# Five u tiles multiplied before the norm is known, x normalised in turned form, and two gate tiles moved ahead of the S5 blocks

## The chip, the core and the metric

The kernel runs on one core of a Trainium2 chip. TensorE (PE) multiplies matrices from SBUF into PSUM, VectorE (DVE) and ScalarE (ACT) work on elements, GpSimd (POOL) fills constants and issues transfers, and SyncE (SP) issues most transfers. The metric is the device time of one execution in microseconds.

Before the change the median of three runs is 883.1 us (883.09 to 883.79).

## The reference

One decoder block works on 16 meta tokens and 512 tokens of width 1024, in fp32. What matters here is its beginning:

```python
h = jnp.concatenate([meta, x], axis=1)
xn = rmsnorm(h, g_mix_pre[l])          # per token: x * rsqrt(mean(x*x) + eps) * g
proj = xn @ w_in[l]                    # q, k, v, r, a_low, u, z_gla, z_ssm
log_a = log_sigmoid(a_low @ w_gate_up[l] + b_gate[l]) / 16
```

The slices of `proj` then go three ways. q, k, v and `log_a` feed a gated linear attention (GLA) with four heads, whose output is normalised, multiplied by silu(r) and by `w_o_gla`. u feeds an S5 state-space layer with 64 groups of 16 channels, followed by gelu and a gated linear unit. Both results are weighted with sigmoid(z_gla) and sigmoid(z_ssm), added, multiplied by `w_out`, and added to h. A squared-ReLU MLP follows.

The norm scales each token by one number, and a product with `w_in` is linear: (s_t x_t g) @ W = s_t ((x_t g) @ W). A projection can so be multiplied first and scaled by the token's number afterwards.

## The kernel before, in words

**How a product is made.** All matrix products keep fp32 precision with three products of a reduced format (fp32r): an operand is split into a high part (a copy on ACT, `split_hi`, line 159) and a low part (the difference, on DVE), and `mm3` (line 186) adds high x high, high x low and low x high over eight blocks of 128 rows, 24 matmuls for an output tile. Weights come as tiles of 1024 x 128 (`wraw`, 512 KB, three buffers), are split by `split_w_hi` and `split_w_lo` into `whi` and `wlo` (three buffers each), and are the stationary operand. The moving operand is the turned, normalised x: `xh` and `xl`, 128 x 8 x 528, features on the partitions and tokens along the line (512 tokens, then the 16 meta tokens). A projection that needs the meta tokens is made in two halves of 256 and 272 tokens (`HALVES`), any other in one piece of 512. Results of projections take the four PSUM buffers named `mm`; everything else takes the four named `sm`.

**The start (lines 276 to 428).** SP loads the meta rows, four x tiles of 128 tokens (`xt`) and the weights of u tiles 0 to 2 in a fixed order. The gain row is spread over the partitions by PE (`gps`, lines 368 to 376). For each x tile ACT sums the squares (`squared`), four small DVE instructions and one of ACT form the inverse root (`rooted`, `rs`), and DVE multiplies by root and gain (`normed`, `xn`). PE turns the tile (`turned`, eight transposes), ACT takes the high part out of PSUM (`high`) and DVE the low part (`low`). `busy(n)` (line 290) lets PE multiply ones. Between these steps stand the first halves of u tiles 0 to 2 (`u_half`, line 255); their second halves follow at line 425. A finished half is copied from PSUM into `ut` by ACT, and `u_out` (line 270) stores the tile to DRAM for the S5 blocks.

**The stage up to S5 (lines 431 to 792).** The low-rank gate product (`low_rank`, line 458, weights `wa`) reads all of `xh` and `xl`; `gate_up` and `decay_sums` make the running sums of `log_a`: DVE subtracts (line 485) and scans against a mask that is zero at each 128th token (line 487). In the same stretch DVE and ACT compute the S5 layer's tables from its parameters (`chain`, `powers`, `chunk_powers`, `b_bar`). Between the steps stand calls of `slot()` (line 500): each takes the next product of the list `dense`, whose weights were asked for two slots before. The list begins with u tiles 3 to 7, z_ssm tiles 0 to 3 and z_gla tile 4 (lines 545 to 549).

**The blocks (lines 1127 to 1200).** Eight S5 blocks follow, each with a small product (`kernels`), a scan over chunks (`scan`) and an output, and five slots between these steps as work for PE. Blocks 0 to 3 are interleaved with the four GLA heads. The list `dense` goes on with each head's tiles, the other z tiles, the r tiles (`r_slot`, line 1097, which leave `ogh` and `ogl`) and the o tiles (`o_slot`, line 1112, which read all eight of them). z_gla tiles 5, 6 and 7 stand among the r tiles and stay in SBUF; tiles 0 to 4 go to DRAM (`zgd`) and are loaded again.

**What sets the order.** PE's instructions stay in program order up to the MLP (`pinned`). In the start, those of DVE and ACT do too (`InOrder`, `V` and `S` up to line 424). All others are placed by a planner that issues what it takes to be ready; `tc.issue_after` puts an instruction behind another one on the same engine. The order of the loads on SP at the start is fixed in this way (`behind`).

Of the kernel before, what the change touches and what calls it, by code (L numbers as in the profile page):

```python
# [12 lines left out]
ALU = mybir.AluOpType  # L13
# [36 lines left out]
def hybrid_block(ctx: ExitStack, tc: tile.TileContext, io, out: bass.AP):  # L50
# [204 lines left out]
    def u_half(w, ut, q, within=None):  # L255

        a, b = HALVES[q]
        ps = bank("mm")
        feat_tile(w, xh, xl, a, b, ps[:, : b - a], within=within)

        def taken():
            src = ps.rearrange("p (c s) -> p s c", s=T8)
            first = NM // T8 + a // T8
            S.copy(ut[:, :, first : first + 32], src[:, :, :32])
            if q:
                S.copy(ut[:, :, : NM // T8], src[:, :, 32:34])

        return taken
# [9 lines left out]
    gpre = mk(pxt, [P, D], tag="gpre")  # L278
    grow = mk(pxt, [1, D], tag="grow")
    one_row = mk(pxt, [1, P], tag="one_row")  # L280
    V.memset(one_row, 1.0)
    nc.scalar.dma_start(grow, io["g_mix_pre"][0].rearrange("(o d) -> o d", o=1))
    xm = mk(pxt, [P, D], tag="xt", bufs=5)
    xts, raws = [], []
    loaded = nc.sync.dma_start(xm[:NM], io["meta_tokens"])
    ones = mk(pxt, [P, 256], tag="ones")
    V.memset(ones, 1.0)
    idle = bank()

    def busy(n):  # L290

        for _ in range(n):
            PE.matmul(idle[:, :256], ones[:, :P], ones, start=True, stop=True)
# [3 lines left out]

    def x_load(t):
        xt = mk(pxt, [P, D], tag="xt", bufs=5)
        xts.append((xt, P, t * P))  # L300
        return nc.sync.dma_start(xt, io["x"][0, t * P : (t + 1) * P, :])


    for kind, i in (("x", 0), ("x", 1), ("u", 0), ("x", 2), ("u", 1), ("x", 3), ("u", 2)):
        with behind():
            if kind == "x":
                loaded = x_load(i)
            else:
                loaded, raw = raw_w(w_in[:, C_U + i * P : C_U + (i + 1) * P])
                raws.append(raw)  # L310
    xts.append((xm, NM, SEQ))
# [3 lines left out]
    nc.gpsimd.dma_start(vecs, io["vecs"])  # L315
    V, S = InOrder(nc.vector), InOrder(nc.scalar)
    ss = mk(pxt, [P, 5], tag="xss")
    rs = mk(pxt, [P, 5], tag="xrs")
    xns = {}

    def squared(i):
        xt, n, _ = xts[i]
        sq = mk(pxt, [P, D], tag="xsq", bufs=1)
        S.activation(sq[:n], xt[:n], AF.Square, accum_out=ss[:n, i : i + 1])

    def rooted(i):

        n = xts[i][1]
        y, ssum = rs[:n, i : i + 1], ss[:n, i : i + 1]
        parts = mk(pxt, [n, 2], tag="xr_r", bufs=3)  # L330
        a, hm = parts[:, :1], parts[:, 1:]
        S.activation(a, ssum, AF.Sqrt, scale=1.0 / D, bias=epst[:n])
        yield
        V.tensor_scalar(hm, ssum, -0.5 / D, -0.5 * EPS, op0=ALU.mult, op1=ALU.add)
        V.reciprocal(y, a)
        V.scalar_tensor_tensor(a, y, hm, y, op0=ALU.mult, op1=ALU.mult)
        V.scalar_tensor_tensor(y, a, 1.5, y, op0=ALU.add, op1=ALU.mult)

    roots = {}

    def summed(i):
        squared(i)
        roots[i] = rooted(i)
        next(roots[i])

    def normed(i, cols=(0, 512)):
        xt, n, _ = xts[i]
        if i not in xns:
            xns[i] = mk(pxt, [P, D], tag="xn", bufs=3)
            next(roots[i], None)  # L350
        xn = xns[i]
        for c in cols:
            cc = slice(c, c + 512)
            V.scalar_tensor_tensor(xn[:n, cc], xt[:n, cc], rs[:n, i : i + 1], gpre[:n, cc], op0=ALU.mult, op1=ALU.mult)

    def turned(i, tag):
        return [turned_tokens(xns[i][: xts[i][1]], xts[i][1], q, tag if isinstance(tag, str) else tag[q]) for q in range(2)]

    def high(i, q, pvs):
        _, n, col = xts[i]  # L360
        split_hi(xh[:, 4 * q : 4 * q + 4, col : col + n], pvs[q])

    def low(i, q, pvs):
        _, n, col = xts[i]
        dst = slice(4 * q, 4 * q + 4)
        V.tensor_sub(xl[:, dst, col : col + n], pvs[q], f32(xh)[:, dst, col : col + n])

    gps = [bank() for _ in range(2)]
    for i, ps in enumerate(gps):
        PE.matmul(ps, one_row, grow[:, i * 512 : (i + 1) * 512], start=True, stop=True)  # L370
    busy(2)
    summed(4)
    V.tensor_copy(gpre[:, :512], gps[0])
    normed(4, (0,))
    summed(0)
    S.copy(gpre[:, 512:], gps[1])
    summed(1)
    normed(0)
    t0 = turned(0, "mm")
    busy(2)  # L380
    normed(1)
    hi0 = split_w_hi(raws[0])
    w0 = hi0, split_w_lo(raws[0], hi0)
    high(0, 0, t0)
    high(0, 1, t0)
    t1 = turned(1, "sm")
    high(1, 0, t1)
    high(1, 1, t1)
    for q in range(2):
        low(0, q, t0)  # L390
        low(1, q, t1)
    ut0, ut1, ut2 = (u_tile() for _ in range(3))
    take0 = u_half(w0, ut0, 0)
    summed(2)
    hi1 = split_w_hi(raws[1])
    w1 = hi1, split_w_lo(raws[1], hi1)
    take1 = u_half(w1, ut1, 0)
    normed(2)
    summed(3)
    hi2 = split_w_hi(raws[2])  # L400
    w2_ = hi2, split_w_lo(raws[2], hi2)
    take0()
    normed(3)
    ts = {}
    take2 = u_half(w2_, ut2, 0, within=(1, lambda: ts.update({2: turned(2, "mm")})))
    high(2, 0, ts[2])
    high(2, 1, ts[2])
    normed(4, (512,))
    low(2, 0, ts[2])
    low(2, 1, ts[2])  # L410
    t4 = turned(4, "sm")
    t3 = turned(3, ("mm", "sm"))
    take1()
    for q in range(2):
        high(4, q, t4)
        low(4, q, t4)
    for q in range(2):
        high(3, q, t3)
        low(3, q, t3)
    take2()  # L420
# [16 lines left out]
    mask01 = mk(pga, [P, NT], tag="mask01")  # L437
    G.memset(mask01, 1.0)
    for c in range(0, NT, P):
        G.memset(mask01[:, c : c + 1], 0.0)  # L440
# [40 lines left out]
    def decay_sums():  # L481
        S.activation(ga, ga, AF.Exp, scale=-1.0)
        S.activation(ga, ga, AF.Ln, bias=1.0)
        for h in range(HEADS):
            V.tensor_sub(mn[:, h], mn[:, h], ga[:, h])
            b2 = mk(pga, [P, NT], tag="b2", bufs=2)
            V.tensor_tensor_scan(b2, mask01, mn[:, h], 0.0, op0=ALU.mult, op1=ALU.add)
            nc.gpsimd.dma_start(bd[h], b2)
# [644 lines left out]
    for kind in ("r0", "r1", "z5", "r2", "r3", "z6", "r4", "r5", "r6", "r7", "z7", *(f"o{m}" for m in range(KT))):  # L1133
# [11 lines left out]
    for b, blk in enumerate(blocks):  # L1145
# [22 lines left out]
        slot()  # L1168
# [20 lines left out]
        slot()  # L1189
# [329 lines left out]
def laid_out(np, given):  # L1519
# [9 lines left out]
    for name, (one, two) in (("b_cols", bt), ("c_cols", ct)):  # L1529
        rows[name] = np.stack([np.concatenate([one, two]), np.concatenate([two, one])])  # L1530
    return {**{name: a[name] for name in _INS}, **rows}
# [26 lines left out]
```

## Time and profile before

| | |
|---|---|
| median of three runs | 883.1 us |
| the profiled execution's own time | 883.62 us |
| its span in the trace | 881.9 us |
| instructions | 13276 |
| TensorE clock granted, mean | 0.997 |
| HBM read and written | 141.06 MB, 35.42 MB |

The page of the profile gives, in this order: busy time of each engine; the span in 40 slices; the DMA queues; the chain of work that ended last, followed back from the last instruction; the costliest groups of instructions by line, engine, operation and tile, written out<-in; and the DMA issues. Other views group instructions by line or window, list what an engine waited for, or show them in order of time. Times are microseconds from the span's start. PE is the matmul row of TensorE and PEld its weight loads. L78 is the helper that keeps DVE and ACT in program order, and L60 and L65 are PE's helpers, so groups are told apart by their tiles. The duration of a matmul in a row includes the time it takes to run through, so the pace of a series is read from the starts.

### The profile page before, as it was taken

What the parts mean: (1) busy time and instruction counts of PE and PEld (TensorE: products, weight loads), DVE (VectorE), ACT (ScalarE), POOL (GpSimd) and SP (SyncE); (2) the same over time, 40 slices, a digit from 0 to 9 for tenths busy, and PEclk for the clock granted to TensorE, in tenths of its full rate; (3) what the DMA queues carried; (4) which work ended last, traced back from release to release, by engine and by line L of the source; (5) the groups of instructions that cost most, each with busy time, mean ns of one, the idle gap of its engine ahead of it and who ended that gap; (6) DMA issues with size and microseconds to landing.
All of it is one profiled execution on the core that took longest, in us unless ns stands there. A gap on an engine that the chain in (4) does not pass through costs nothing.

```text
span 881.9 us, 13276 instructions
## 1 busy us (share of the span) xinstructions
PE 869.5 (99%) x4856; PEld 742.5 (84%) x4856; DVE 648.6 (74%) x1148; ACT 437.7 (50%) x731; POOL 124.0 (14%) x224
## 2 busy tenths in 40 slices
PE   8999999999999999999999999999999999999996
PEld 6998989898988888888888888988888888888885
DVE  7989898868778698755445765576666678788886
ACT  6475466767655454434333543333222236665763
POOL 1223022030312213232000001021112100000001
PEclk9999999999999999999999999999999999999998
DMA  9647785555454857558545761589998966856564
GB/s 305 179 126 239 205 196 143 136 134 161 109 166 126 260 130 176 170 161 274 187 143 160 228 178 57 172 288 324 333 305 298 324 244 224 280 190 194 170 209 142
DMA packets 164988, 177.36 MB, mean 201 GB/s; under 512 B 18778, under 2 KB 125306, under 8 KB 164923
## 3 DMA queue, kind: packets, MB, share of 16 engines
q1 hardware_dynamic: 146056, 114.74, 44.8%
q0 software_dynamic: 17696, 57.84, 19.4%
q10 hardware_dynamic: 1170, 3.94, 1.3%
q8 instruction: 38, 0.62, 0.3%
q14 instruction: 28, 0.22, 0.1%
HBM read 141.06 MB, written 35.42 MB: 200 GB/s over the span
## 4 chain that ended last, share of the span: by engine, by line
PE 96%; DVE 2%; ACT 1%; DMA 0%; issue 0%; DVEq 0%; SPq 0%
PE mm L60 73%; PE sm L60 21%; PE sm L65 2%; DMA xt<-in_x_dram 0%; DVE xn L78 0%; DVE wlo L78 0%; ACT xsq L78 0%; DVE c L1483 0%; DVE xl L78 0%; PE mm L65 0%; DVE ede L604 0%; DVE c L1477 0%; ACT xh L78 0%; ACT whi L78 0%; DVEq L1554 0%
## 5 line engine op out<-in xcount | busy, mean ns | idle before, releaser
L160 ACT ACTIVATE whi<-wraw 128x1024 fp32r<-128x1024 f32 x101 | 107.0, 1059 | 236.1 <-PE mm L60 207.9
L175 DVE TENSOR_TENSOR wlo<-wraw,whi 128x1024 fp32r<-128x1024 f32 x101 | 123.4, 1222 | 106.7 <-ACT whi L160 106.5
L60 PE MATMUL mm<-xh,whi 128*128 128x512 f32 (+2 forms) x544 | 182.2, 335 | 0.5 <-ACT xh L78 0.5
L60 PE MATMUL mm<-xl,whi 128*128 128x512 f32 (+2 forms) x544 | 178.6, 328 | 1.1 <-DVE xl L78 1.1
L60 PE MATMUL mm<-xh,wlo 128*128 128x512 f32 (+2 forms) x544 | 178.9, 329 | 0.2 <-DVE wlo L78 0.2
L60 PEld LDWEIGHTS mm<-xh,whi 128*128 128x128 f32 x544 | 102.7, 189 | 10.6 <-issue 1.2
L60 PEld LDWEIGHTS mm<-xl,whi 128*128 128x128 f32 x544 | 102.8, 189 | 10.0 <-DVE xl L78 1.5
L60 PEld LDWEIGHTS mm<-xh,wlo 128*128 128x128 f32 x544 | 102.6, 189 | 9.7 <-DVE wlo L78 0.6
L60 PE MATMUL mm<-hh,whi 128*128 128x512 f32 (+1 forms) x280 | 104.0, 371 | 0.0
L60 PE MATMUL mm<-hl,whi 128*128 128x512 f32 (+1 forms) x280 | 103.8, 371 | 0.0
L60 PE MATMUL mm<-hh,wlo 128*128 128x512 f32 (+1 forms) x280 | 103.8, 371 | 0.0
L1420 DVE TENSOR_TENSOR wlo<-wraw,whi 128x1024 fp32r<-128x1024 f32 x56 | 68.4, 1222 | 20.2 <-ACT whi L1416 20.0
L60 PE MATMUL sm<-wlo,fh 128*128 128x512 f32 x192 | 74.8, 390 | 0.0
L60 PE MATMUL sm<-whi,fl 128*128 128x512 f32 x192 | 74.7, 389 | 0.0
L60 PE MATMUL sm<-whi,fh 128*128 128x512 f32 x192 | 74.7, 389 | 0.0
L1416 ACT ACTIVATE whi<-wraw 128x1024 fp32r<-128x1024 f32 x56 | 58.6, 1048 | 17.2 <-PE mm L60 11.7
L60 PEld LDWEIGHTS mm<-hl,whi 128*128 128x128 f32 x280 | 52.7, 188 | 9.1
L60 PEld LDWEIGHTS mm<-hh,whi 128*128 128x128 f32 x280 | 52.7, 188 | 9.1
L60 PEld LDWEIGHTS mm<-hh,wlo 128*128 128x128 f32 x280 | 52.7, 188 | 8.9
L160 ACT ACTIVATE fh<-f 128x512 fp32r<-128x512 f32 x48 | 30.3, 631 | 45.7 <-PE sm L60 30.6
L60 PE MATMUL mm<-gh,whi 128*128 128x512 f32 x128 | 49.8, 389 | 0.0
L60 PE MATMUL mm<-gl,whi 128*128 128x512 f32 x128 | 49.8, 389 | 0.0
(415 smaller groups left out, 1635.0 us busy)
## 6 DMA issues: line engine op xcount, KB each, us to landing
wraw<-in_w_ff_dram SPq DMA_DIRECT2D x56, 512.0 KB, 4.4
wraw<-in_w_in_dram SPq DMA_DIRECT2D x48, 512.0 KB, 4.1
w2raw<-in_w_ff_dram POOLq DMA_DIRECT2D x16, 1024.0 KB, 8.5
t2d<-w2t POOLq DMA_DIRECT2D x16, 1024.0 KB, 5.8
wraw<-t2d SPq DMA_DIRECT2D x32, 512.0 KB, 3.8
wraw<-in_w_glu_dram SPq DMA_DIRECT2D x16, 512.0 KB, 4.4
M<-kpad POOLq DMA_DIRECT2D x64, 64.0 KB, 2.6
wraw<-in_w_o_gla_dram SPq DMA_DIRECT2D x8, 512.0 KB, 7.9
```

What stands on the lines that cost most here:

```text
L60: ins = nc.tensor.matmul(*args, **kw)
L65: ins = nc.tensor.transpose(*args, **kw)
L160: S.activation(dst, src, AF.Copy, scale=scale)
L175: V.tensor_sub(lo, raw, f32(hi))
L1416: halved = S.activation(bh, raw, AF.Copy)
L1420: V.tensor_sub(bl, raw, f32(bh))
```

## The change

**The start.** The kernel receives x and the meta tokens a second time, already turned (`x_cols0` holds the first 256 tokens, `x_cols1` the rest, features on the partitions), and the gain as columns (`g_cols`). The turned x times the gain is split into `rh` and `rl` (`taken_raw`): ACT writes the high part, DVE the low part. u tiles 0 to 4 are multiplied from these. The x tiles by rows are still loaded, three buffers instead of five, for the sums of squares alone. Their roots are formed in two groups (x tiles 0 and 1; then 2, 3 and meta). `spread` brings a group's roots onto all partitions as a row: ACT makes a diagonal matrix of each column, PE multiplies it with ones, and ACT copies the sum. A finished half of a u tile is multiplied by this row on DVE as it leaves PSUM (`taken`), where ACT copied it before. Turned x is then normalised by column tile (`normed`): DVE multiplies by gain and row, ACT copies the high part, and DVE subtracts for two column tiles at once. PE no longer turns x, and the gain is no longer spread. `busy` runs seven matmuls at the start. u tile 0's weights are loaded and split in pieces.

**Decay sums.** The mask is gone. The scan adds one operand and subtracts the other, and is cut at each 128th token, five scans for a head where there was one scan and one subtraction.

**Slots.** `dense` begins with u tiles 5 to 7, z_ssm tiles 0 to 3 and z_gla tiles 4 to 6, ten entries as before. z_gla tiles 5 and 6 are so computed before the blocks, go to DRAM, and are loaded again at o tiles 5 and 6. Among the r tiles only z tile 7 is left, between r6 and r7. The last S5 block has two slots fewer.

```diff
-    def u_half(w, ut, q, within=None):
+    def u_half(w, ut, q, raw=None, tag="mm", within=None):
...
+                if raw:
+                    V.tensor_mul(to, got, scale_rows[0].rearrange("p (c s) -> p s c", s=T8)[:, :, a // T8 + c : a // T8 + c + n])
+                else:
+                    S.copy(to, got)
...
+    for kind, i in (("u", 1), ("h", 0), ("h", 4), ("x", 0), ("x", 1), ("u", 2), ("x", 2), ("x", 3), ("x", 4), ("u", 3), ("u", 4)):
...
+    def taken_raw(k, a, b):
+
+        g = g8[:, k : k + 1]
+        S.activation(rh[:, k, a:b], xT[:, k, a:b], AF.Copy, scale=g)
+        V.scalar_tensor_tensor(rl[:, k, a:b], xT[:, k, a:b], g, f32(rh)[:, k, a:b], op0=ALU.mult, op1=ALU.subtract)
...
+    def spread(c, cols):
+
+        ps = bank()
+        for j, i in enumerate(range(c.start, c.stop)):
+            n = xts[i][1]
+            dg = mk(pxt, [P, P], tag="diag", bufs=3)
+            S.activation(dg[:n, :n], ident[:n, :n], AF.Copy, scale=rs[:n, i : i + 1])
+            PE.matmul(ps[:, j * P : j * P + n], ones[:n, :P], dg[:n, :n], start=True, stop=True)
+        S.copy(rows[:, cols], ps[:, : cols.stop - cols.start])
+
+    def normed(k):
+        V.scalar_tensor_tensor(xT[:, k], xT[:, k], g8[:, k : k + 1], rows, op0=ALU.mult, op1=ALU.mult)
+        S.copy(xh[:, k], xT[:, k])
+        if k % 2:
+            V.tensor_sub(xl[:, k - 1 : k + 1], xT[:, k - 1 : k + 1], f32(xh)[:, k - 1 : k + 1])
...
+    busy(7)
...
+    product(0, 0, w0)
+    w1 = split_w(raws[1])
+    product(1, 0, w1)
+    for k in range(KT):
+        taken_raw(k, 256, NT)
+    product(0, 1, w0)
+    product(1, 1, w1)
+    early, late = slice(0, 2), slice(2, TT + 1)
+    squared(0)
+    squared(1)
+    rooted(early)
+    w2_ = split_w(raws[2])
+    spread(early, slice(0, 256))
+    take(0, 0)
+    take(1, 0)
+    for i in range(2, TT + 1):
         squared(i)
...
+    rooted(late)
+    product(2, 0, w2_)
+    spread(late, slice(256, NT))
+    take(0, 1)
+    take(1, 1)
+    w3 = split_w(raws[3])
+    product(2, 1, w2_)
+    take(2, 0)
+    for i in range(2):
+        u_out(i, uts[i])
+    uts.extend(u_tile() for _ in range(2))
+    product(3, 0, w3)
+    product(3, 1, w3)
     normed(0)
...
     normed(1)
...
+    take(2, 1)
+    u_out(2, uts[2])
+    w4 = split_w(raws[4])
+    for k in range(2, KT):
+        normed(k)
+    product(4, 0, w4)
+    product(4, 1, w4)
+    for i in (3, 4):
+        for q in range(2):
+            take(i, q)
+        u_out(i, uts[i])
     wa = mk(pg, [P, KT, 32], F32R, tag="wa")
     split_hi(wa[:, :, :16], wraw)
     begun = V.tensor_sub(wa[:, :, 16:], wraw, f32(wa)[:, :, :16])
     V, S = nc.vector, nc.scalar
-    for blk, w, ut in ((0, w0, ut0), (1, w1, ut1), (2, w2_, ut2)):
-        u_half(w, ut, 1)()
-        u_out(blk, ut)
...
-            V.tensor_sub(mn[:, h], mn[:, h], ga[:, h])
             b2 = mk(pga, [P, NT], tag="b2", bufs=2)
-            V.tensor_tensor_scan(b2, mask01, mn[:, h], 0.0, op0=ALU.mult, op1=ALU.add)
+            for c in range(0, NT, P):
+                cc = slice(c, min(c + P, NT))
+                V.tensor_tensor_scan(b2[:, cc], mn[:, h, cc], ga[:, h, cc], 0.0, op0=ALU.add, op1=ALU.subtract)
...
-    for m in range(3, KT):
+    for m in range(5, KT):
         u_slot(m)
     for m in range(4):
         gate_slot(C_ZS, m, zs, early_tile)
-    gate_slot(C_ZG, 4, zg, early_tile)
+    for m in range(4, 7):
+        gate_slot(C_ZG, m, zg, early_tile)
...
-    for kind in ("r0", "r1", "z5", "r2", "r3", "z6", "r4", "r5", "r6", "r7", "z7", *(f"o{m}" for m in range(KT))):
+    for kind in ("r0", "r1", "r2", "r3", "r4", "r5", "r6", "z7", "r7", *(f"o{m}" for m in range(KT))):
...
-        slot()
+        if b < NBLK - 1:
+            slot()
```

More of the change, by code (lines that the diff above doesn't have):

```diff
@@ L307, in hybrid_block @@
                 loaded = x_load(i)
+            elif kind == "h":
+                loaded = nc.sync.dma_start(xT[:, i : i + 4, 256:], io["x_cols1"][:, i : i + 4])
             else:
@@ L321, in squared @@
     def squared(i):
[L322 to L334, printed above, removed]
+        xt, n = xts[i]
@@ L356, in turned @@
[L356 to L370, printed above, removed]
@@ new lines, in normed, with product, take @@
+    def normed(k):
[3 more added lines that the diff above has]
+            V.tensor_sub(xl[:, k - 1 : k + 1], xT[:, k - 1 : k + 1], f32(xh)[:, k - 1 : k + 1])
+    raw = rh, rl
+    uts = [u_tile() for _ in range(3)]
+    takes = {}
+    def product(i, q, w, within=None):
+        takes[i, q] = u_half(w, uts[i], q, raw, within=within)
+    def take(i, q):
+        takes[i, q]()
+    busy(7)
@@ new lines, in hybrid_block @@
+    w0 = tuple(mk(wp, [P, KT, P], F32R, tag=t, bufs=3) for t in ("whi", "wlo"))
+    for k in range(0, KT, 2):
+        kk = slice(k, k + 2)
+        for i in range(2):
+            taken_raw(k + i, 0, 256)
+        split_hi(w0[0][:, kk], raws[0][:, kk])
+        V.tensor_sub(w0[1][:, kk], raws[0][:, kk], f32(w0[0])[:, kk])
+    product(0, 0, w0)
[5 more added lines that the diff above has]
+    product(1, 1, w1)
@@ L378, in hybrid_block @@
+    product(3, 0, w3)
+    product(3, 1, w3)
     normed(0)
-    t0 = turned(0, "mm")
-    busy(2)
     normed(1)
[L382 to L416, printed above, removed]
```

108 lines of the change are left out of this document (51 added, 57 removed).

## The prediction

> **What bounds the kernel now.** I read the page's first and fourth parts, then the waits of PE, then windows, then the first 50 us in order of time. Busy time and the chain that ended last, from the page:
>
> ```profile
> PE 869.5 (99%) x4856; PEld 742.5 (84%) x4856; DVE 648.6 (74%) x1148; ACT 437.7 (50%) x731; POOL 124.0 (14%) x224
> ...
> PE 96%; DVE 2%; ACT 1%; DMA 0%; issue 0%; DVEq 0%; SPq 0%
> ```
>
> PE's waits over the whole span (us in total, times, longest):
>
> ```profile
> PE sm L60 <- DMA grow<-in_g_mix_pre_dram: 2.6, 1, 2.6
> PE mm L60 <- DVE xl L78: 1.1, 2, 0.7
> PE mm L60 <- ACT xh L78: 0.5, 2, 0.3
> ```
>
> PE is the bound, and each of these waits lies in the first 28 us. A gain can therefore come only from the start; everywhere later a change can only add a wait. Windows of the start and of the end (length, busy us of PE, PEld, DVE, ACT and POOL, clock, DMA share, GB/s):
>
> ```profile
> 0.00:4.60 4.60, 1.95 (x3) 0.94 (x4) 0.88 (x8) 2.93 (x5) 3.35 (x12) 1.00 0.49 143
> 0.00:8.00 8.00, 5.35 (x8) 2.34 (x8) 3.77 (x19) 5.36 (x10) 3.35 (x12) 1.00 0.73 240
> 8.00:13.00 5.00, 4.82 (x20) 3.98 (x20) 4.76 (x10) 2.92 (x7) 0.00 (x0) 1.00 1.08 372
> 14.00:46.00 32.00, 30.46 (x244) 28.88 (x245) 29.91 (x121) 17.26 (x38) 6.40 (x17) 1.00 0.69 208
> 874.00:881.90 7.90, 0.18 (x1) 0.00 (x0) 3.61 (x9) 0.98 (x3) 1.06 (x2) 0.64 0.44 133
> ```
>
> The start is no PE stage: from 14 to 46 us DVE is busy 29.9 of 32 us, nearly as much as PE. PE in order of time (start, duration):
>
> ```profile
> 8.58 1.94 PE L65 MATMUL mm<-ident,xn 128*128 128x128 f32 x8 [0.18 <-DVE xn L78]
> ...
> 21.17 1.03 PE L65 MATMUL mm<-ident,xn 128*128 128x128 f32 x8
> ...
> 36.70 0.28 PE L60 MATMUL mm<-xh,wa 128*32 128x256 f32 x1
> ...
> 40.52 0.28 PE L60 MATMUL mm<-xh,whi 128*128 128x256 f32 x1
> ...
> 46.40 0.64 PE L60 MATMUL sm<-alow,wgr 96*128 96x256 f32 x4
> ...
> 104.10 0.45 PE L60 MATMUL sm<-M,BA 128*32 128x128 f32 x8
> ```
>
> The low-rank gate product (`wa`) begins at 36.70, with three u tiles done; u tile 3 runs from 40.52 to 46.40, so a u tile is 5.88 us, two are 11.76. That gives the yardstick: the new kernel does five u tiles before the same product, so it breaks even if `wa` begins at 36.70 + 11.76 = 48.46.
>
> **The change, part by part.** Prices of DVE and then ACT, 4 to 30 us (count | busy us, mean ns):
>
> ```profile
> L78 DVE SCALAR_TENSOR_TENSOR xn<-xt,xrs,gpre 128x512 f32<-128x512 f32 x8 | 5.6, 746 | 0.1
> L78 DVE TENSOR_TENSOR wlo<-wraw,whi 128x1024 fp32r<-128x1024 f32 x3 | 3.7, 1220 | 0.9 <-ACT whi L78 0.9
> L78 DVE TENSOR_TENSOR xl<-mm,xh 128x512 fp32r<-128x512 f32 x5 | 3.3, 677 | 0.0
> L78 DVE TENSOR_TENSOR xl<-sm,xh 128x512 fp32r<-128x512 f32 x3 | 2.1, 684 | 0.7 <-ACT xh L78 0.7
> L604 DVE SCALAR_TENSOR_TENSOR ede<-ede,edr 128x64 f32<-128x64 f32 x5 | 2.0, 403 | 0.1
> ```
>
> ```profile
> L78 ACT ACTIVATE xsq<-xt 128x1024 f32<-128x1024 f32 x4 | 4.2, 1054 | 1.2 <-DMA xt<-in_x_dram 1.2
> L78 ACT ACTIVATE whi<-wraw 128x1024 fp32r<-128x1024 f32 x3 | 3.1, 1042 | 0.0
> L78 ACT ACTIVATE xh<-mm 128x512 fp32r<-128x512 f32 x5 | 2.9, 597 | 2.5 <-PE mm L65 2.5
> ```
>
> *Loads.* By 4.6 us 143 x 4.6 = 0.66 MB have moved; the meta rows and the first x tile are 0.59 MB, and the first square of x waits until about 5.5: some 0.9 us from last byte to user. By 8.0 us 1.92 MB, then 0.372 MB/us. Ahead of u tile 1's weights the new order has half of turned x (1.05 MB) and two weight tiles (0.52 MB each): 2.10 MB, at 8.5, used at 9.4. The packets are shorter than those of x's rows, so I take 9.8.
>
> *First four raw products.* Product (0,0) runs while its pieces arrive and is done by about 10. Tile 1's weights: 1.04 on ACT and 1.22 on DVE, so the low part stands at 12.1. Of product (1,0) 22 of 24 matmuls are left, 2.7; (0,1) and (1,1) are 3.0 each: PE is at 20.8. The splits of the second half of raw x (eight on each engine) fit beside this. This is where the gain should come from: before, the first such product began at 13.6.
>
> *The norm's rows.* ACT's copy of the early row waits for PE's row product, which stands behind (1,1): 20.8 + 0.5 + 0.35 = 21.7. Behind it on ACT stand three squares (x tiles 2, 3 and meta) of 1.05, each with the short read of its sum, 1.2 together: 25.3; the root, one ACT and five small DVE instructions, 1.3: 26.6; diagonals, row products and the copy, 1.7: 28.3.
>
> *DVE from there to `wa`,* pinned in order: eight takes at 0.35 (half of an `xl` with its fixed part) with five 16-column pieces of 0.13, 3.4; two weight low parts, 2.3; eight normalisations of 528 columns at 0.70, 5.6; four `xl` of 1056 columns at 1.17, 4.7; four waits of 0.7, since each `xl` pair wants ACT's 0.6 us copy made after the normalisation just ahead of it, 2.8; `wa`'s own low part, 0.3. Sum 19.1: DVE ends at 47.4 and `wa` begins at 47.5. PE alone would be free at 42.8 (the last row product at 28.0, half a u tile of 3.0, two whole tiles of 11.8). **Term 1: 47.5 - 48.46 = -1.0 us.** Its lower end is PE not waiting, -5.7; its upper +2, if DVE's list is a tenth slower.
>
> *S5's own DVE work* is not pinned and is placed in the gaps that the planner sees. Before, such instructions (`ede`, mean 403 ns where 200 is usual) stood ahead of `xl`, and PE waited 1.1 us for `xl`. **Term 2: +0.5,** between 0 and 1.1.
>
> *The clock.* PE now idles from 42.8 to 47.5. In the last window PE is busy for 0.18 us only and the mean granted clock is 0.64: full clock held for 2.2 us after the last matmul (0.28 x 7.9), half after. At the start, eight transposes take 1.94 us at 8.58 and 1.03 at 21.17: half pace. About 4 us of dense PE work passed before full pace, so half a clock for 4 us costs 2. **Term 3: +1.9,** between 0 (the clock stays) and +4 (twice as long).
>
> The Trainium skill, "TensorE: Matmul & The Clock Gate", Part 1, has the same direction: half clock after an idle window of some 3.4 us, full again after a busy one. By its 3.4 us the loss would be 1.7, an estimate, and the time 885.0; an idle stretch well below a window would cost nothing by it. The trace agrees on the halving, and shows the drop sooner, at 2.2 us; the page calls the window free-running.
>
> *Two z tiles ahead of S5* change PE's work by nothing: they are computed once, earlier. A z tile is 5.47 (three such tiles in 16.42, below). The first S5 matmul comes at 47.5 + 67.4 - 11.76 + 2 x 5.47 = 114.1 instead of 104.10, and it did not wait before. DVE's added work ahead of it is 5.8 (raw low parts, 16 x 0.36) + 4.2 (ten takes) + 5.6 + 4.7, less 5.6 (eight `xn`), 5.4 (the `xl` rows above) and 2.8 (four decay subtractions):
>
> ```profile
> L487 DVE TENSOR_TENSOR_SCAN b<-mask,mn 128x528 f32<-128x528 f32 x4 | 5.0, 1242 | 0.0
> ...
> L485 DVE TENSOR_TENSOR mn<-mn,ga 128x528 f32<-128x528 f32 x4 | 2.8, 689 | 1.3 <-ACT ga L483 1.3
> ```
>
> That is 6.5 us against 10 of new time; the four scans are cut into twenty over the same columns, about 5 us as before. Price 0. Also at 0: x loaded twice (2.1 MB, 5.7 us of the queue; u tile 3's weights then come near 21, wanted at 28), x tile 3's load, which waits on SP for the first square, and the two z stores on POOL and their loads on SP, which meet the product only where it is multiplied on DVE, behind four PSUM buffers.
>
> *The last r tile* now stands right ahead of the first o tile, which reads all eight; before, a z tile stood between. PE, then DVE, around the r tile in the same place after block 6's scan:
>
> ```profile
> 349.44 0.39 PE L60 MATMUL mm<-xh,wlo 128*128 128x512 f32 x1
> 349.67 0.39 PE L60 MATMUL mm<-xh,whi 128*128 128x512 f32 x1
> ```
>
> ```profile
> 356.70 0.68 DVE L1108 TENSOR_TENSOR ogl<-rs,ogh 128x512 fp32r<-128x512 f32 x1
> ```
>
> Its product ended at 349.67 and its low part at 357.4, 7.7 later; the o tile wants it at its 23rd matmul, 5.0 later. By the row PE waits 2.7; but a z tile stands ahead now where an r tile stood, and 3 x 0.69 of DVE work goes. **Term 4: +0.7,** between 0 and 2.7.
>
> *The last S5 block* loses two slots of cover between its scan and its output. The chain, and DVE's last step of the scan:
>
> ```profile
> 374.81 1.73 PE sm L60 x16
> 376.54 16.42 PE mm L60 x72
> ```
>
> ```profile
> 383.37 0.69 DVE L1054 TENSOR_TENSOR X<-X,vs 128x520 f32<-128x520 f32 x1
> ```
>
> X stands at 384.1; with two slots left PE comes at 376.5 + 2 x 5.47 + 0.4 = 387.8. Price 0.
>
> **The sum.** -1.0 + 0.5 + 1.9 + 0.7 = +2.1 us. The profiled execution took 883.62 (span 881.9), so 885.7; it lies 0.5 above the median of 883.1, so 885.2. Under 0.2% (1.8 us) counts as no change.
>
> **Rivals.** (a) *The move comes to nothing:* the clock does not fall (the idle stretch is cut short, or the low-rank product is fast anyway) and the other terms stay: -1.0 + 0.5 + 0.7, 883.3. For it: a wait of 0.7 us at 27.7 cost no clock. Against: 2.2 us was enough at the end.
> (b) *It does what it says, faster:* PE reaches `wa` with a wait under 2 us, since DVE's list closes before 45; then the clock holds too: about 44.5 - 48.5 + 0.7 = -3.3, 879.8; with no wait 878. It decides at a `wa` start of 45. For it: DVE has some 8 us of gaps between 14 and 28 that could take S5's work. Against: from 28 on the list is one engine's sum in measured prices, and gaps before do not shorten it.
> (c) *DVE closes later, and the r tile's wait is full:* `wa` at 49, clock 3, r tile 2.7: 0.5 + 3 + 2.7 = +6, 889. For it: DVE was 93% busy here already.
>
> **How the numbers follow.** Forecast 0.43 (its own range 883.8 to 887.5), (a) 0.26, (b) 0.17, (c) 0.14. Faster by 0.2% (below 881.3): all of (b) and a quarter of (a), 0.24. Same: most of (a) and a fifth of the forecast, 0.28. Slower: the rest, 0.48. The range leaves out half of (b) and less than half of (c): 879.8 to 889.5.
>
> **What would show it.** Right: no transposes of x; first product ending near 10; `wa` near 47.5 behind DVE's `wa`; idle before it over 4 us; a window clock below 1.00 there; a PE wait on `ogl` near r tile 7. Wrong: `wa` before 45; PE waiting in 100 to 130 us; a clock of 1.00 throughout.

## The result: 896.8 us, 1.5% slower, and where the 13 us went

The changed kernel takes 896.8 us in the median (895.17 to 896.99) against 883.1; the ratio is 1.0152, with a 95% interval of 1.0134 to 1.0169. The forecast was 885.2, at most 889.5. The direction was right, the size was not. From the page of the changed kernel, busy time and the chain that ended last:

```profile
PE 870.2 (97%) x4828; PEld 742.6 (83%) x4828; DVE 655.4 (73%) x1175; ACT 440.3 (49%) x734; POOL 125.7 (14%) x220
...
PE 86%; DVE 7%; ACT 2%; DMA 2%; issue 1%; POOL 1%; SPq 0%; DVEq 0%; ACTq 0%; POOLq 0%
```

PE's busy time is as large as before (870.2 against 869.5, half-clock stretches included), but PE idles 24.9 of 895.1 us where it idled 12.4, and a tenth of the chain has left PE. PE's waits between 50 and 425 us, where before there was none:

```profile
PE sm L60 <- DVE mn L488: 1.8, 2, 1.0
PE mm L60 <- ACT ogh L160: 1.5, 1, 1.5
PE sm L65 <- DVE e_gk L885: 0.9, 1, 0.9
PE mm L60 <- DVE wlo L175: 0.7, 1, 0.7
PE mm L60 <- DVE ogl L1119: 0.6, 1, 0.6
```

Marks of the chain (start, length): the first S5 matmul, block 6's product, and the last turning of S5's output, first of the kernel before, then of the changed one:

```profile
104.17 0.59 PE sm L60 x16
...
334.39 2.49 PE sm L60 x48
406.47 0.44 PE sm L65 x4
```

```profile
123.13 0.59 PE sm L60 x16
...
354.21 2.49 PE sm L60 x48
...
419.71 0.44 PE sm L65 x4
```

With the two z tiles moved forward (10.94 us of PE) the first two marks should stand at 115.1 and 345.3, the last at 406.5. The loss is 8.0 us by the first, 8.9 by the second, 13.2 by the third, and nothing behind that. In the windows of the changed kernel (length, busy us of PE, PEld, DVE, ACT, POOL, clock, DMA share, GB/s) the clock is halved three times:

```profile
42.33:46.82 4.49, 0.00 (x1) 0.00 (x0) 3.67 (x4) 2.52 (x5) 0.00 (x0) 1.00 0.00 0
46.82:53.64 6.82, 4.03 (x19) 2.97 (x20) 6.29 (x15) 0.36 (x1) 4.62 (x7) 0.50 0.57 159
53.64:70.71 17.07, 15.27 (x121) 14.40 (x119) 11.82 (x56) 7.79 (x19) 4.13 (x8) 1.00 0.63 185
70.71:74.12 3.41, 3.41 (x19) 3.41 (x18) 3.41 (x15) 3.30 (x3) 0.00 (x0) 0.50 0.31 92
74.12:377.91 303.79, 300.08 (x2018) 262.50 (x2018) 259.26 (x532) 175.95 (x329) 66.27 (x119) 1.00 0.63 169
377.91:381.32 3.41, 3.41 (x10) 2.62 (x9) 3.34 (x7) 0.69 (x1) 0.57 (x1) 0.50 0.20 80
```

PE in order of time around the three places:

```profile
42.05 0.28 PE L60 MATMUL mm<-rh,wlo 128*128 128x272 f32 x1
49.61 0.39 PE L60 MATMUL mm<-xh,wa 128*32 128x256 f32 x1 [7.28 <-DVE wa L78]
...
67.76 0.41 PE L60 MATMUL sm<-alow,wgr 96*128 96x256 f32 x2
69.00 0.38 PE L60 MATMUL sm<-alow,wgr 96*128 96x256 f32 x1 [0.83 <-DVE mn L488]
70.36 0.39 PE L60 MATMUL sm<-alow,wgr 96*128 96x272 f32 x1 [0.97 <-DVE mn L488]
70.59 0.30 PE L60 MATMUL mm<-xh,whi 128*128 128x256 f32 x1
...
375.86 0.49 PE L60 MATMUL mm<-ogh,whi 128*128 128x512 f32 x1 [1.45 <-ACT ogh L160]
377.01 0.50 PE L60 MATMUL mm<-ogl,whi 128*128 128x512 f32 x1 [0.65 <-DVE ogl L1119]
```

| place | loss, us | from |
|---|---|---|
| `wa` at 49.61 instead of 48.46 | 1.15 | its row |
| low-rank product at half clock | 1.9 | half of the 4.03 us that PE ran in the first half-clock window, and its pace: 5.7 us to u tile 5 instead of 3.8 |
| `gate_up(2)`, `gate_up(3)` wait for `mn` | 2.2 | 67.76 to 70.59 is 2.8, the four took 0.64 before |
| half clock behind that | 1.5 to 1.7 | 3.41 us at half pace |
| weights late at 106.5; GLA's keys late at 144.9 | 0.7 + 0.9 | the waits |
| last r tile ahead of the first o tile | 2.5 | the o tile's 23rd matmul begins at 377.01; at the pace of its first ones it would have at 374.5. The two waits are 2.1 of it |
| half clock behind that | 1.7 | 3.41 us at half pace |

That is 12.6 to 12.8 of 13.2 us; about half a us I did not locate.

The waits for `mn` have a cause far ahead of them. The S5 constants start from one small load, `ab`, issued by POOL. POOL's work before, and in the changed kernel (start, duration), and the chain's first instruction on DVE there:

```profile
2.95 0.56 POOL L582 DMA_DIRECT2D ab<-in_a_step_dram  x1
```

```profile
48.44 0.54 POOL L280 DMA_DIRECT2D ud<-ut  x1 [12.46 <-DVE ut L78]
49.56 0.54 POOL L280 DMA_DIRECT2D ud<-ut  x1 [0.57 <-DVE wa L78]
50.09 0.55 POOL L451 MEMSET trif<- 128x512 f32 x1
...
52.72 2.52 POOL L458 DMA_DIRECT2D wgu<-in_w_gate_up_dram  x5
55.23 0.58 POOL L593 DMA_DIRECT2D ab<-in_a_step_dram  x1
```

```profile
L597 DVE TENSOR_SCALAR ab<-ab x1: 196/196/196, 60.0 to 60.0; 128x64 f32<-128x64 f32 x1
```

The turned x and its raw halves are larger than what they replace. The pool of the S5 constants (`q5`) is laid out from the right end of SBUF, the start's pool (`pxt`) from the left, and now they overlap; `ab` waits until `pxt` is released, near 49.5, and then stands behind POOL's mask and the `wgu` issues until 55.2 (e2 shows that the overlap is the reason). The chain that ran from 17.7 us runs from 60, in the same stretch as `gate_up`, the decay sums and the weights' splits. The gaps of DVE between 15 and 28 us, which I had counted for it, stayed empty.

### The profile page after: what moved, and what is told of

Read it like the earlier page. It is cut to its first block, busy times and chain, and to the rows that moved or that the text cites. A ratio compares the mean times of both kernels' runs of the same rounds, so it can differ in the third digit from the quotient of the medians.

```text
span 895.1 us, 13259 instructions
## 1 busy us (share of the span) xinstructions
PE 870.2 (97%) x4828; PEld 742.6 (83%) x4828; DVE 655.4 (73%) x1175; ACT 440.3 (49%) x734; POOL 125.7 (14%) x220
## 4 chain that ended last, share of the span: by engine, by line
PE 86%; DVE 7%; ACT 2%; DMA 2%; issue 1%; POOL 1%; SPq 0%; DVEq 0%; ACTq 0%; POOLq 0%
PE mm L60 63%; PE sm L60 21%; PE sm L65 2%; DVE wlo L175 1%; DMA wraw<-in_w_in_dram 1%; DMA wgu<-in_w_gate_up_dram 1%; DMA U<-ud 1%; DVE xT L78 1%; DVE wlo L78 0%; DVE ut L78 0%; DVE b L497 0%; ACT xt L78 0%; DVE xl L78 0%; ACT xh L78 0%; DVE v L1060 0%
## 5 line engine op out<-in xcount | busy, mean ns | idle before, releaser
L160 ACT ACTIVATE whi<-wraw 128x1024 fp32r<-128x1024 f32 x99 | 104.9, 1059 | 239.1 <-PE mm L60 203.8
L175 DVE TENSOR_TENSOR wlo<-wraw,whi 128x1024 fp32r<-128x1024 f32 x99 | 120.9, 1221 | 103.2 <-ACT whi L160 101.1
L60 PE MATMUL mm<-xh,whi 128*128 128x512 f32 (+2 forms) x464 | 159.6, 344 | 0.0
L60 PE MATMUL mm<-xh,wlo 128*128 128x512 f32 (+2 forms) x464 | 156.7, 338 | 0.7 <-DVE wlo L175 0.7
L60 PE MATMUL mm<-xl,whi 128*128 128x512 f32 (+2 forms) x464 | 156.4, 337 | 0.0
L60 PEld LDWEIGHTS mm<-xh,wlo 128*128 128x128 f32 x464 | 88.2, 190 | 10.2 <-DVE wlo L175 1.1
L60 PEld LDWEIGHTS mm<-xh,whi 128*128 128x128 f32 x464 | 88.3, 190 | 9.5 <-issue 1.0
L60 PEld LDWEIGHTS mm<-xl,whi 128*128 128x128 f32 x464 | 88.3, 190 | 8.4
L1433 DVE TENSOR_TENSOR wlo<-wraw,whi 128x1024 fp32r<-128x1024 f32 x56 | 68.4, 1223 | 20.0 <-ACT whi L1429 19.9
L1429 ACT ACTIVATE whi<-wraw 128x1024 fp32r<-128x1024 f32 x56 | 58.6, 1049 | 16.8 <-PE mm L60 11.7
```

The costliest lines, as they stand in the source:

```text
L60: ins = nc.tensor.matmul(*args, **kw)
L160: S.activation(dst, src, AF.Copy, scale=scale)
L175: V.tensor_sub(lo, raw, f32(hi))
L1429: halved = S.activation(bh, raw, AF.Copy)
L1433: V.tensor_sub(bl, raw, f32(bh))
```

## The experiments

Ratios are to the kernel before, with their 95% intervals; a difference in us is the ratio's part above 1 times 883. The changed kernel stands at +13.4.

**e1, the slots' order.** In the list: `"r6", "z7", "r7"` becomes `"r6", "r7", "z7"`.

> Only the slots' order changes: z tile 7 stands behind r tile 7 again, as in the kernel before. Theory A (of the 13.4 us lost, 4.3 come from the last r tile standing right ahead of the first o tile: PE waits 1.5 us for ogh and 0.6 for ogl at 375 to 377 us and then runs 3.4 us at half clock): both waits go, the clock stays 1.00 there, and the time falls by 4.3, 896.8 to about 892.5. Rival B (DVE is crowded by block 6's scan there, whatever stands ahead of the o tile): the wait only moves behind the z tile, the time falls by under 1.5.

Measured 892.1, 1.0099 (1.0084 to 1.0114): 4.7 us back. Between 355 and 425 us PE waits for nothing, and the clock stays:

```profile
355.00:400.00 45.00, 45.00 (x254) 37.57 (x253) 37.32 (x60) 17.96 (x31) 14.24 (x26) 1.00 0.67 191
```

Theory A holds.

**e16, the same adjacency in the kernel before.** `"r7", "z7"` becomes `"z7", "r7"` there.

> The kernel before with z tile 7 ahead of r tile 7, so that r7 stands right ahead of o0, and nothing else. If adjacency alone costs it: DVE and ACT need some 7.5 us from r7's last product to ogl and PE is there after 5: a wait of 2 to 2.7 us, a stretch of half clock behind it of 1.7, together 4 us, 887. If it takes block 6's scan beside it on DVE (in the changed kernel r7 stands behind that scan's matmuls, here two tiles later): a wait under 1 us, no half clock, at most 884.

Measured 883.8, 1.0011 (1.0002 to 1.0021), +1.0 us. The one new wait:

```profile
PE mm L60 <- DVE ogl L1108: 0.7, 1, 0.7
```

So adjacency alone costs a wait of 0.7 (1.0 in the median). In the changed kernel z tiles 5 and 6 are gone from among the r tiles, r7 comes two slots sooner, and its product begins right behind block 6's scan matmuls; the end of that scan, a weight split and two table instructions stand among r7's own on DVE, and `ogl` ends at 376.95, 7.7 us behind the start of r7's last matmul at 369.26. The wait became 2.1, enough for the clock to fall. It is one part of the change that makes another part dear.

**e2, the S5 constants out of the start's reach.**

```diff
+    qc = pool("qc", stack=st5, side="right")
     q5 = pool("q5", stack=st5, side="right")
-    nat = mk(q5, [P, 7, N], tag="nat")
+    nat = mk(qc, [P, 7, N], tag="nat")
...
```

(and so for `ab` and the chain's small tiles)

> The S5 constants' input ab, nat and the chain's small tiles are taken from a pool of their own on the right, which the normalisation's tiles do not reach; nothing else changes. Theory C (ab's load was issued at 55.2 us instead of 3.0 because its memory was the normalisation's until 49.9, so the chain ran in 60 to 79 us, ahead of gate_up's mn on DVE): ab lands by 10 us, the two waits at 69.0 and 70.4 go (2.2 us), so does the half clock at 70.7 to 74.1 (1.5 us), and the waits at 106.5 and 144.9 (0.7 and 0.9) at least shrink: 3.7 to 5.3 us less, 896.8 to about 892. Rival D (DVE is crowded in 50 to 80 us by the weights' splits anyway): ab lands early and the waits stay, under 1 us less. Rival E: the chain's work wedges itself into DVE's list before wa, which then begins later than 49.6 and takes 1 to 2 us back.

Measured 893.5, 1.0116 (1.0097 to 1.0136): 3.2 us back. `ab` is issued at 2.9 us and its chain starts at 13. The waits for `mn` and `e_gk` and the second half clock are gone. But `wa` begins at 51.48, 1.9 later than in the changed kernel. Theory C holds, rival E in part. About 0.6 of the 1.9 comes from the loads: with `ab`'s load beside them the first weights land later, and the low part of u tile 1's weights begins at 11.48 instead of 10.91. Some 1.1 more arises since the chain stands ahead of the norm's late roots (ACT waits 1.88 for them, 0.83 in the changed kernel). From the late row on, DVE's list takes as long as before (29.74 to 51.05 against 28.05 to 49.18): there the chain fitted into the waits for `xh` and lengthened nothing. A wait of 0.8 for `wlo` between 90 and 100 us remains, so the 0.7 at 106.5 in the changed kernel is not shown to come from the lateness.

**e7 and e9, late constants in the kernel before.** In e7 the load of `ab` was put behind `wa`'s low part by order of issue; that orders only one engine, `ab` was still issued at 3.0, and the time was the same (1.0001, 0.9991 to 1.0010). It tried nothing.

> The kernel before, with the load of ab held on POOL until DVE has made wa's low part (36.7 us instead of 3.0); wgu's loads and the u tiles' stores stand behind it on POOL. It puts into the kernel before what theory C says of the changed kernel. Theory C: gate_up's mn wait on DVE behind the chain and PE waits 2 to 4 us between 45 and 110 us, 883.1 to 885 or 887. Rival D (DVE has room for the chain wherever it stands): under 0.7 us.

e9 makes the load wait for data:

```diff
+    with tc.issue_after(begun.ins):
+        V.memset(ab[:, 0, :1], 0.0)
     nc.gpsimd.dma_start(ab, io["a_step"])
```

> e7's order of issue left ab's load at 3.0 us, so e7 tried nothing. Here one small DVE write into ab stands behind wa's low part, and the load has to wait for it: ab is issued near 37 us in the kernel before, and its chain starts near 42 instead of 17.7. Theory C (late constants cost PE waits by themselves): 1 to 4 us more than 883.0. Rival D (between 42 and 104 us DVE has room for the chain, and only the tighter spacing of the changed kernel, 60 to 115, turns lateness into waits): under 0.7 us.

Measured 892.5, 1.0100 (1.0080 to 1.0120), +8.8 us. The load was issued at 32.5 and its chain began at 36.6, 19 us late. From the waits of PE, then from DVE in order of time, then the clock:

```profile
PE mm L60 <- DVE wlo L175: 7.5, 1, 7.5
```

```profile
100.22 1.23 DVE L762 TENSOR_TENSOR M<-M,prm 128x1024 f32<-128x1024 f32 x1 [7.86 <-DMA M<-in_b_cols_dram]
...
104.24 1.22 DVE L175 TENSOR_TENSOR wlo<-wraw,whi 128x1024 fp32r<-128x1024 f32 x1
```

```profile
100.64:110.88 10.24, 5.37 (x25) 5.37 (x26) 10.24 (x17) 4.25 (x6) 0.54 (x1) 0.50 0.52 151
```

Theory C holds, twice as dear as I had it, and by another road: late constants make the load of B's columns late (issued at 87.4 instead of 73.0; its pool opens where the constants' pool was), DVE stands still for it 7.9 us, and the weights' low part for the next slot stands behind it.

**e3, filling PE's idle stretch.**

```diff
     product(4, 1, w4)
+    fill = bank()
+    for _ in range(15):
+        PE.matmul(fill[:, :256], ones[:, :P], ones, start=True, stop=True)
```

> Fifteen idle matmuls of 256 columns are put behind u tile 4's product, in the stretch from 42.4 to 49.6 us in which PE has nothing to do. Theory F (PE's idle stretch is what halves the clock for the low-rank product): no half clock at 46.8 to 53.6, the low-rank product takes about 3.8 us instead of 5.7, and the time falls by 1.9, to about 895, if what follows (gate_up's weights, ready at 61.2) is not late then. If it is, the 1.9 us turn into a wait ahead of gate_up(0) and the time stays at 896.8. Rival G (the half clock has another cause): the clock is halved all the same.

Measured 896.8, 1.0145 (1.0117 to 1.0173), nothing gained. Windows of it, and the new waits:

```profile
42.20:49.70 7.50, 6.64 (x32) 5.53 (x31) 6.46 (x12) 2.74 (x5) 0.58 (x2) 1.00 0.01 4
49.70:61.50 11.80, 9.87 (x80) 9.10 (x80) 5.59 (x13) 2.36 (x6) 7.06 (x11) 1.00 1.00 282
61.51:68.34 6.83, 5.96 (x28) 5.96 (x29) 6.42 (x25) 2.98 (x8) 0.55 (x1) 0.50 0.33 95
```

```profile
PE sm L60 <- DVE wgr L468: 2.8, 1, 2.8
PE mm L60 <- DVE wlo L175: 2.5, 1, 2.5
```

Theory F holds: the clock stays full, u tile 5 begins at 53.5 instead of 55.3. Then `gate_up(0)` waits 2.8 us for its weights, whose load stands behind the same memory on POOL, and the clock falls there instead.

**e4, `wa` split early** (behind u tile 3's weights).

> The split of wa moves from the end of DVE's list to behind u tile 3's weights, so that the low-rank product can begin at 42.4 and follow the normalisation column by column; the takes of u tiles 3 and 4 come after. Theory H (gate_up's weights, whose loads stand behind the normalisation's memory on POOL's queue and were split at 61.2, are the next to be late): the low-rank product ends by 51 instead of 55.2 and u tile 5 by 57, but gate_up(0) still begins at 61, and the time falls by under 1 us. Rival I (nothing stands behind it): the 4 us come through, to about 892.5.

Measured 896.0, 1.0147 (1.0126 to 1.0168), nothing gained. The low-rank product began at 47.15, 2.5 sooner (it waited for u tile 3's takes, which hold its PSUM buffers). `gate_up(0)` then waited 1.6 for `wgr`, and a slot at 117 waited 3.9 for `wlo`. Theory H holds.

**e5, e6 and e10: the repairs together.** e6 is e1 with e2 and `wgu` in the pool `qc`; e5 is e6 with e4; e10 is e6 with the chain's first steps held behind `wa` on DVE.

> The edits of e1, e2 and e4 together, and the gate weights' input wgu also in the pool that the normalisation's tiles do not reach. Theory J (the losses are separate: 4.7 of the slots' order, 3.3 of the late constants, and 4 us that the early wa could not bring in while gate_up's weights and the constants were late): 896.8 - 4.7 - 3.3 - 4 = about 885, within 2 us of the kernel before. Rival K (with everything early DVE becomes the wall, since the constants' chain then stands among the normalisation's instructions): wa's product is paced by it, the low-rank product ends near 55 as before, and the time is about 889.

> As e5, but wa's split stays at the end of DVE's list. Theory J: the two gains of e1 and e2 add, 896.8 - 4.7 - 3.3 = 888.8, and wgu's earlier load adds nothing, since wgr was ready at 61.2 when gate_up(0) came. Rival K: about 890 or more, wa still later than 51.5.

> e6 with the chain's first two steps issued behind wa's low part on DVE: the constants are loaded by 10 us but their chain starts at about 50, neither among the normalisation (e6) nor at 60 (the changed kernel). If the wedged chain is what made wa 2 us later in e6 than in the changed kernel: wa at 49.6 again and 890.2 - 2 = about 888. If the lateness costs as much as the wedging, 890 to 892, with waits at gate_up or ahead of the first S5 matmul.

e6 890.2, 1.0083 (1.0060 to 1.0105); e5 893.6, 1.0113 (1.0092 to 1.0133); e10 890.1, 1.0078 (1.0063 to 1.0093). e6 is 1.8 above the sum of the gains of e1 and e2 (7.3 us above the kernel before, where 13.4 - 4.7 - 3.2 is 5.5), within its interval. e10 does no better in the median, but it tells more. Its chain starts at 55.4, behind `wa`, and yet PE waits for only 0.2 us between `wa` (51.11) and the first S5 matmul: the waits that I had feared did not come. What keeps it slow lies ahead of `wa`. With the loads of `wgu` and `ab` (0.29 MB) issued from 3 to 6 us, beside those of the first weights, the weights land 7.4 us after their issue instead of 5.9. The low part of u tile 1's weights, in the changed kernel and in e10:

```profile
10.91 1.23 DVE L78 TENSOR_TENSOR wlo<-wraw,whi 128x1024 fp32r<-128x1024 f32 x1 [0.67 <-ACT whi L78]
```

```profile
12.41 1.23 DVE L78 TENSOR_TENSOR wlo<-wraw,whi 128x1024 fp32r<-128x1024 f32 x1 [1.43 <-ACT whi L78]
```

These 1.5 us reach the takes behind the late row (29.55 instead of 28.05) and so `wa`. In e10's profiled execution `wa` is 2.65 us behind break-even (48.46), the low-rank product takes 6.0 instead of 3.8 under a half clock of 6.82 us from 49.1, and the waits are 0.2: about 5.0, as much as its span is longer (886.9 against 881.9). In all of e5, e6 and e10 to e15 these weights are 1.2 to 1.6 us late, in every run that loads `wgu` and `ab` late within 0.1 of the changed kernel; no run moves the two loads back in the repaired kernels, so what that would save is not tested. e5's `wa` product begins at 53.21, but its clock was halved from 12.3 to 19.2 us in the profiled execution and its takes behind the late row began at 32.55 (28.07 in e4), so it does not show rival K.

**e11, e12 and e15: an early low-rank product.** e11 is e10 with e4 and the low-rank product in the `sm` buffers; e12 adds a sixth raw u tile; e15 is e12 with the chain left to the planner.

> e10 with wa's split early (as e4) and the low-rank product in the other PSUM banks, since in e4 it waited for the takes of u tile 3 and not for the normalisation. It should then start near 43 and follow the normalisation, u tile 5 starts near 51 instead of 55.3: 4 us below e10, about 884. If the next thing late is the constants' chain (a wait ahead of gate_up or the first S5 matmul), less than 2 us.

> e11 with a sixth raw u tile: PE has 5.9 us more to do while DVE normalises, so it does not idle between 42.3 and 48 and the clock is not halved. By the yardstick the low-rank product with six u tiles ahead breaks even at 36.7 + 17.6 = 54.3 and should begin near 49: 5 us below the kernel before there. One slot less lies between it and S5. If the S5 constants are ready: about 879 to 881, faster than the kernel before. If they are late (a PE wait of some us between 95 and 125 us), 884 to 888.

> e12 without holding the constants' chain behind the normalisation, so that it fills DVE's gaps from 15 us on. If DVE's total work is the wall, filling the 8 us of gaps helps: the waits for wlo shrink from 8.9 to about 4 us while the low-rank product is some 2 us later: 887 to 889. If the chain's place does not matter: 890.6 as e12.

e11 890.3, 1.0088 (1.0070 to 1.0107); e12 890.6, 1.0084 (1.0069 to 1.0099); e15 887.6, 1.0054 (1.0036 to 1.0072). The start did gain in e11 and e12: `wa` at 43.44, and at 50.16 with six u tiles, 4.2 under that kernel's break-even of 54.34. All of it and more is paid back before the first S5 matmul, which begins at 120.99 in e11 and 122.07 in e12, where 115.1 would be even. DVE between the two, in the kernel before and in e12:

```profile
36.70:104.10 67.40, 67.40 (x450) 61.98 (x448) 61.82 (x146) 37.86 (x69) 12.87 (x22) 1.00 0.65 191
```

```profile
50.16:122.00 71.84, 62.89 (x354) 54.30 (x352) 67.75 (x216) 36.60 (x59) 16.46 (x27) 0.98 0.65 185
```

Already before, DVE was busy 61.8 of 67.4 us there, 92%; in e12 it is 94%, and PE waits 8.9 us for `wlo`. In e15 the chain fills gaps from 15 us on, PE waits 4.1, and the first S5 matmul comes at 119.96, but `wa` is back at 54.33. Of these 4.2 us against e12, 2.8 come from a clock halved from 12.85 to 19.7 us in the profiled execution and not from the chain: u tile 1's 25th raw matmul began at 22.00 instead of 19.17. That is the best of these kernels, still 0.5% slower than the kernel before.

**e13 and e14: 12 us of tables on POOL.** `powers`, `b_bar` and `b_cols` of e6 and of e15 use `G` instead of `V`.

> e6 with the powers of lambda, B-bar and the scaling of B's columns (27 instructions, some 12 us on DVE) moved to POOL. If DVE's work is the wall between the low-rank product and the first S5 matmul: in e6 PE hardly waits there (0.7 us), so the time falls by under 1 us from 890.2. If POOL's instructions, slower and ahead of DMA issues on POOL's queue, hold up the loads: 891 to 895.

> e15 with the same 12 us moved from DVE to POOL. If DVE's work is the wall: the PE waits for wlo of e15 (8 us expected there) shrink to under 3 us, and the time is 4 to 6 us below e15, about 884 to 886. If the loads are the wall: as e15.

e13 906.4, 1.0262 (1.0246 to 1.0277); e14 904.7, 1.0248 (1.0231 to 1.0265). POOL in e13, and the same product on DVE in the changed kernel:

```profile
L759 POOL TENSOR_TENSOR bta<-bn,fb 128x512 f32<-128x512 f32 x2 | 3.4, 1709 | 0.1
L773 POOL TENSOR_TENSOR BA<-BA,M 128x1024 f32<-128x1024 f32 x1 | 2.4, 2404 | 0.1
```

```profile
L758 DVE TENSOR_TENSOR bta<-bn,fb 128x512 f32<-128x512 f32 x2 | 1.4, 688 | 0.5 <-ACT fb L752 0.5
```

Both came out slower than either theory allowed. POOL takes two to two and a half times as long (2404 ns for `BA`, 1207 to 1217 on DVE; 1709 for `bta`, 688 on DVE), the chain goes through it, and PE waits 7.7 us for `mn` in e13 and 12.6 for one `wlo` in e14. So these two do not tell whether DVE without that work would have been fast enough. That DVE is the limit there stays argued, from the 92% and 94%, and e10, with 0.2 us of waits in the same stretch, is an example against it.

**e8 and e17, the decay sums.** e8 is e1 with the old sums, e17 the kernel before with the new ones:

```diff
-            V.tensor_sub(mn[:, h], mn[:, h], ga[:, h])
-            V.tensor_tensor_scan(b2, mask01, mn[:, h], 0.0, op0=ALU.mult, op1=ALU.add)
+            for c in range(0, NT, P):
+                cc = slice(c, min(c + P, NT))
+                V.tensor_tensor_scan(b2[:, cc], mn[:, h, cc], ga[:, h, cc], 0.0, op0=ALU.add, op1=ALU.subtract)
```

> e1 with the decay sums of before (one subtraction and one masked scan for a head instead of five pieces of scan). The prediction put the change of the decay sums at 0. By that e8 equals e1, 892.1, within 0.7. Rival: 2.8 us of DVE work more in 75 to 95 us make the late constants later still, and the time is 1 to 3 us above e1; or the twenty short scans cost more than they save, and it is 1 us below.

> The kernel before with the new decay sums alone (twenty pieces of scan in place of four subtractions and four masked scans; the mask's memsets go). The prediction put it at 0: 883.1 within 0.7. Rival: the planner puts DVE's work around it in another order, as in e8, and it moves by a microsecond or more either way.

e17 884.6, 1.0017 (1.0007 to 1.0026), +1.5 us. DVE's scans in it:

```profile
L484 DVE TENSOR_TENSOR_SCAN b<-mn,ga 128x128 f32<-128x128 f32 x16 | 5.9, 409 | 6.0 <-DMA bd<-b 4.7 <-ACT ga L479 1.3
```

Cutting a scan into pieces of 409 ns (four are 1.64, the whole one is 1.24) takes back 1.6 of the 2.8 us of the saved subtractions (the pieces sum to 6.6, whole scans to 5.0), and the scans waited 4.7 us for the store of an earlier head's buffer; PE waited 1.4 us for `wlo`. e8 took 901.3, 1.0204 (1.0189 to 1.0219), 9 us above e1, where I had allowed 3 at most: in the changed kernel the old sums are dearer, in the kernel before the new ones. As in e9 DVE stood 8.0 us for the load of B's columns, and a weight's low part behind it held PE 10.6. Whether the sums alone do that or the order that the planner found with them, these runs do not tell.

## Why the prediction was wrong

The sum forecast +2.1 us; +13.4 was measured. The step that failed most is term 2: it took the S5 constants to be loaded early and priced only the place of their work ahead of `wa`, at 0.5; they came at 60 us, and that cost about 4.6. Terms 1 and 4 had the right mechanism and were too small, by 2.1 and by 3.5 to 4. Term 3 was right.

- *Loads, first four products, rows:* right. The low part of tile 1's weights stood at 12.1, the late row at 28.0 (28.3 said), PE's part of the list ended at 42.3 (42.8).
- *Term 1, -1.0:* it was +1.15. The list of DVE from 28 us, grouped:

```profile
L78 DVE SCALAR_TENSOR_TENSOR xT<-xT,g,xrows 128x528 f32<-128x528 f32 x8 | 5.8, 761 | 0.0
L78 DVE TENSOR_TENSOR xl<-xT,xh 128x1056 fp32r<-128x1056 f32 x4 | 5.0, 1258 | 3.6 <-ACT xh L78 3.6
L78 DVE TENSOR_TENSOR ut<-mm,xrows 128x256 f32<-128x256 f32 x8 | 4.9, 631 | 2.0 <-ACT xrows L78 2.0
L78 DVE TENSOR_TENSOR wlo<-wraw,whi 128x1024 fp32r<-128x1024 f32 x2 | 2.4, 1211 | 0.0
L78 DVE TENSOR_TENSOR ut<-mm,xrows 128x16 f32<-128x16 f32 x5 | 0.8, 168 | 0.0
```

  The takes failed: I priced 256 columns at 0.35 from an `xl`, and reading PSUM by phases takes 0.63. Their busy time is 5.7 where I had 3.4; counted from start to start, since the ends overlap, they fill 4.8 of the list, 1.4 too much. The waits for `xh` are 3.6 in place of 2.8, one of 1.5 where ACT split the next weights first. Together that is about the 2.1.
- *Term 2, +0.5 for S5's work among the list:* the mechanism was wrong in this kernel. The work did not wedge itself in, since its data came at 60 us. I had not looked at where `ab`'s memory lies. Lateness cost some 4.6 us (waits of 2.2 and 0.9, half clock of 1.5). e2 brought back 3.2 net and lost 1.9 at `wa`: some 1.1 to the chain's place ahead of the roots, 0.6 to later weights, and nothing to the list itself, which term 2 had priced. A late chain is not dear as such: in e10 it starts at 55.4 and PE hardly waits; what differs there is that `wgu` was loaded early too, and which of the two matters these runs do not separate.
- *Term 3, +1.9:* right, 1.9. One reading under it does not fit: the clock column that the prediction shows says 1.00 for 8 to 13 us, so the half pace of the eight transposes at 8.58 rests on their durations alone. And e3 shows that the term was worth nothing by itself, since `gate_up`'s weights were next. I had not asked what was late behind it.
- *Term 4, +0.7 of at most 2.7:* 0.7 is what e16 measured for the kernel before; here it was 2.1 of wait (2.5 by the matmuls' starts) and 1.7 of half clock, 4.7 by e1. The row that I had quoted said 2.7, and I talked it down. The upper end left out the clock, which I had priced earlier.
- *Price 0 for the z tiles and DVE's added work:* the comparison of 6.5 us with 10 us of new time failed. What counts is when DVE can do the work. That a stage in which it is busy 92% gives none back is argued from e11 and e12 (4.5 and 8.9 us of waits for `wlo`), and e10 is an example against it. *Price 0 for the decay sums:* 1.5 in the kernel before; in the changed kernel e8 has the other sign.
- *The upper bound:* the range ended at 889.5 since it summed single waits. Each of the waits at 69, 106, 145 and 376 us came from a step priced at 0 or 0.7, and the clock then added 1.5 to 1.7 to two of them.

## What to carry to other kernels

When tiles at the start grow, check which pools they now overlap: a load of 96 KB moved from 3 to 55 us, and in the kernel before a delay of 30 us on that load cost 8.8 us. Look also at which loads the early small ones run beside: the first weights came 0.6 us later in e2 and 1.5 in e10. A stage in which the second engine is busy 90% may have no room for work that comes late (8.9 us of waits in e12, 0.2 in e10), so price a moved chain by the stage that it lands in, not by the sum. And to every wait of some 2 us on PE add what the clock may take behind it.

## What the runs showed of the hardware

The half-clock stretches last 3.41, 6.82 or 10.24 us, whole multiples of 3.41; the same idle stretch of 7.3 us ahead of `wa` gave 6.82 in the changed kernel and 10.24 in e1. Their starts lie on one grid: in the changed kernel (70.71 - 46.82) / 7 and (377.91 - 46.82) / 97 are both 3.413. The Trainium skill, "TensorE: Matmul & The Clock Gate", Part 1, gives a free-running window of 3413 ns, and the trace agrees. From the end of the kernel before I had read that full clock holds 2.2 us into an idle stretch (2.0 from the last matmul's end at 874.18); here it held 4.5 (42.33 to 46.82), and 3.1 in e1. By a free-running window all three can be.

The fall needs no window without work. In the changed kernel PE was busy for 0, 1.61 and 1.40 us of the 3.41 us ahead of the three falls. At the last place 2.1 us of waits with one matmul between them (374.4 to 377.0) were enough, while in e12 a wait of 2.0 at 87.5 us cost no clock: it lay across an edge of the grid (86.6) and left PE busy for 2.31 and 2.53 us on the two sides. No single share fits all runs: in e15 a window with 65% of PE's time busy (9.44 to 12.85) was followed by a fall, one with 49% (101.60 to 105.02) was not. So the threshold stays open. Full clock came back in the changed kernel after a window in which PE never paused (50.22 to 53.64); in e1 the window from 48.89 to 52.31 was busy for 76%, and the clock came back only behind the next one, which was full (52.31 to 55.72).
